# Ties in the order of work in five places of a two-layer diffusion step, and end states scaled and stored in place

## The chip, the cores and the metric

The kernel runs on one core of one Trainium2 chip. The core has five engines that each work through a queue of their own in order: TensorE (PE in the profile; PEld is its weight load), VectorE (DVE), ScalarE (ACT), GpSimd (POOL) and SyncE (SP), which here issues most of the DMAs. The metric is the device time of one execution in microseconds (us); lower is better.

## The reference

One denoising step of a backbone with two layers over 256 context tokens and 1024 latent tokens of width 1024. Layer 0 mixes tokens with gated linear attention (a scan in both directions, 4 heads, chunks of 64), layer 1 with softmax attention (8 heads, 2 key heads, normed queries and keys, rotary positions on latent tokens). Both layers are normed, modulated by a condition, gated and added to the residual. Besides the tokens it returns the end states of the context's scans and the context's keys and values. Cut to what matters:

```python
for l in range(DEPTH):
    mod_p = (silu(c_ctx) @ w_ada[l] + b_ada[l])
    mod_s = (silu(c) @ w_ada[l] + b_ada[l])
    hp = rms_norm(xp, norm_g[l]) * (1 + sc_p) + sh_p        # context; hs likewise for latent tokens
    if l % 2 == 0:
        out_p, st = gla_mixer(hp, ..., s_zero)              # st: end state of each direction and head
        out_s, _ = gla_mixer(hs, ..., state_gla)            # scans start from given states
    else:
        qp, kp, vp, gp = attn_project(hp, ...)              # k = rms_norm(k, knorm), no rotary
        out_p = (attend_blocks(qp, kp, vp) * silu(gp)) @ w_out
        out_s = (attend_blocks(rope(qs), [rope(ks), cache_k], [vs, cache_v]) * silu(gs)) @ w_out
    xp, xs = xp + gt_p * out_p, xs + gt_s * out_s
```

## The kernel before, in words

Tokens come in ten tiles of 128 rows: tiles 0 and 1 are the context, 2 to 9 the latent tokens. Every product of full precision is made of three products of 16-bit halves (`mm3`, L130): high by high, high by low, low by high. So each operand is first scaled by a power of two (`pow2`, from a maximum) and split into `hi` (ScalarE) and `lo` (VectorE).

**Who sets the order.** The text of the program is a list of instructions for each engine; before the run a planner lays out each engine's order with a timing model of its own (`schedule_with_timeline_sim`, L54), and semaphores then hold every instruction until its data are there. An instruction that stands early in its engine's order and has to wait for data holds up all behind it. `with tc.issue_after(ins):` puts every instruction of the block that runs on the engine of `ins` behind `ins` in that engine's order. It adds no wait on other engines, and instructions of the block on other engines, DMAs of SP among them, are not tied.

**The scan of layer 0** (`gla`, L824) runs 50 slots: head by head, tile by tile, forward for even heads and backward for odd ones. Each slot projects values and gates, does the work inside a chunk (`intra`), the outer product and running state (`outer`, `scan`), and for the head before it the other direction (`combine`). The running state W is a tile of a pool with two buffers (`Wa`, `Wc`). At the last context tile of a direction `final_state` (L737) scales W into the tile `s0`, which has one buffer, and ScalarE's queue stores it. The same `s0` receives the given state at the start of a scan (L727) and pieces of the gate's bias (L399). In the profile `s0` appears as `s`.

`filler` (L1558) adds other work to the slots: weights for later, and from slot 40 the output product of layer 0. `fold_gate` (L897) loads the gate vectors of a layer (two DMAs) and multiplies them by the weight's scale (eight instructions on POOL); it runs at slot 40. From slot 40 the mixed rows are loaded again in the order 2 to 9, 0, 1 (`ROWS`); `row_parts` (L928) takes a row's maximum, splits the row and turns it by DMA. Rows 2 to 7 are multiplied during the scan, at the slots of `EARLY` = 43 to 47 and 49 (`row_out`): each output tile has two halves, in the PSUM banks `A` and `kt`. `residual` (L908) evacuates a half on VectorE with two instructions: L916 scales it in the bank, L917 adds the residual to it.

**Between the layers** (`gla_out`, L943) rows 8, 9, 0 and 1 are multiplied (banks `y`), and the rows of layer 1 are normed (`norm`), turned (`turn`, banks `tr`), modulated, and made into keys and values (`key_tile`, L1122, banks `kv`). Beside that go scales of layer 1 (`att_setup`) and quarters of its output weight: `out_part` loads one into `st`, and `fill(0)` and `fill(1)` take its maxima and split it. `key_tile` norms the keys (`head_norm`), splits and turns them (`split_transpose`, with the split in the two-buffered tile `xhl`). For the two context tiles, the last of all, it also stores the keys and values.

**Attention** (`attention`, L1276) has ten steps (two groups of four heads by five chunks of 256 queries); the context chunk is the fifth in each group's first round. Each of the four heads of a step makes two blocks of scores: three-bank tiles `S`, two of them; VectorE takes the maximum (L1183, kept as `self.last`), ScalarE the exponential (L1188), POOL and VectorE split it, SP turns it into `PT`. Two heads later `values` multiplies it and L1245 evacuates it. Queries are projected two per step, ahead. In the tenth step the first output chunk is loaded, scaled and split (`out2_load`, `out2_scale`, `out2_parts`), and the first output tile multiplied in between; `att_out` (L1363) does the other nine tiles, and prepares one chunk (`out2_prep`) while the one before is multiplied. `out_tile` (L1352) loads the residual `x1_d` just ahead of its products.

Of the kernel before, what the change touches and what calls it, by code (L numbers as in the profile page):

```python
# [57 lines left out]
IDLE = (5, 9)  # L58
TURNED = 4

class K:
# [675 lines left out]
    def final_state(self, h, d, st):  # L737
        o = self.t(self.ew, [P, DV], F32, "s0", bufs=1)
        self.nc.vector.tensor_scalar(o, st["W"], st["eb"][:, d, 1:2], None, ALU.mult)
        self.nc.scalar.dma_start(self.O[2][0, 0, d, h], o)  # L740
# [75 lines left out]
    def gla_init(self):  # L816
        self.qkt = self.t(self.qkp, [P, 2 * T], F32, "qk")
        self.qk = [[[None] * 3, [None] * 3] for _ in range(GH)]
        self.inv_qk = [None, None]
        self.inv_v, self.inv_g = [None] * GH, [None] * GH  # L820
        self.v = [[None] * NT for _ in range(GH)]
        self.jobs, self.open = [], []
# [74 lines left out]
    def fold_gate(self, l, inv, gt):  # L897
        nc = self.nc
        self.gt = gt
        for i in range(2):  # L900
            nc.sync.dma_start(gt[:, i, :], self.gt_d[l, i : i + 1, :].to_broadcast([P, D]))
        for b in range(4):
            for i in range(2):
                g = gt[:, i, 256 * b : 256 * b + 256]
                nc.gpsimd.tensor_scalar(g, g, inv[b], 1.0, ALU.mult, ALU.mult)


    def residual(self, i, lhs, wo, inv, x, banks=None, cuts=(512, 512), out=None):  # L908
# [3 lines left out]
        for j, n in enumerate(cuts):  # L912
            ps = (banks[j] if banks else self.bank("y"))[:, 0:n]
            self.pieces(ps, lhs, wo, b, n)
            a = slice(b, b + n)
            nc.vector.scalar_tensor_tensor(ps, ps, inv, g[:, a], ALU.mult, ALU.mult)  # L916
            nc.vector.tensor_tensor(x[:, a], ps, x[:, a], ALU.add)  # L917
            if out is not None:
                nc.scalar.dma_start(out[:, a], x[:, a])
# [8 lines left out]
    def row_parts(self, i, parts):  # L928
        nc, og = self.nc, self.row.pop(i)
        mx = self.t(self.small, [P, 1], F32, "wm1")  # L930
        nc.vector.tensor_reduce(mx, og, AX.X, ALU.max, apply_absolute_value=True)
# [11 lines left out]
    def gla_out(self, wo, wkv):  # L943
# [32 lines left out]
        self.o1 = []  # L976
# [8 lines left out]
        with self.tc.issue_after(self.scaled):  # L985
            self.att_setup(*ckv)
# [6 lines left out]
        fill(0)  # L993
# [128 lines left out]
    def key_tile(self, i, w):  # L1122
# [4 lines left out]
        x = self.t(self.hw, [P, 2, HD], F32, "hx")  # L1127
        nc.scalar.activation(x.rearrange("p h d -> p (h d)"), ps[:, 0:256], AF.Copy, scale=self.inv_k)
        self.head_norm(x, self.kn, x)
# [3 lines left out]
        if i < NTP:  # L1133
            nc.scalar.dma_start(self.O[3][0, 0, i * P : i * P + P], x)
            v = self.t(self.hw, [P, 2, HD], F32, f"pv{i}", bufs=1)
            nc.scalar.activation(v.rearrange("p h d -> p (h d)"), pv, AF.Copy, scale=self.inv_av)
            nc.scalar.dma_start(self.O[4][0, 0, i * P : i * P + P], v)
        else:
            self.rope(x, i)
        a = slice(j * P, j * P + P)  # L1140
        self.split_transpose(x, self.asc[:, 1:2], self.kT[:, :, a])
# [91 lines left out]
    def values(self, h, c, PT, g):  # L1233
# [11 lines left out]
        nc.vector.scalar_tensor_tensor(og, o, g[1], g[0], ALU.mult, ALU.mult)  # L1245
# [30 lines left out]
    def attention(self, wo):  # L1276
# [3 lines left out]
        for n, (p, c) in enumerate(self.steps):  # L1280
# [6 lines left out]
            for e in range(4):  # L1287
# [18 lines left out]
                if n == 9 and e == 0:  # L1306
                    row = self.out2_load(OUT[0])
# [9 lines left out]
        self.out_tile(OUT[0], 0, self.t(self.sp, [P, TS + PAST], F32, "p")[:, 0:D], wo)  # L1317
        row = self.out2_load(OUT[1])
        self.second = row, *self.out2_scale(row)
        for t in pend:  # L1320
            self.values(*t, g.pop(t[0]))

# [29 lines left out]
    def out_tile(self, c, j, x, wo, cuts=(512, 512)):  # L1352
        hi, lo, inv = self.prep
        i, a = 2 * c + j, slice(j * P, j * P + P)
        self.nc.sync.dma_start(x, self.x1_d[i])
# [48 lines left out]
def emit(ctx, tc, I, O, dbg=None, stop=None):  # L1404
# [31 lines left out]
    with ExitStack() as c:  # L1436
# [119 lines left out]
        wo, part, held, rows, parts, xs, waiting = [None] * 4, [], [], [], [], [], []  # L1556

        def filler(slot):  # L1558
            if part:
# [202 lines left out]
```

## Time and profile before

| | us |
|---|---|
| median of 3 runs | 1268.66 (1267.31 to 1269.15) |
| the profiled execution | 1266.46 |
| its span | 1264.7 |
| scan and what precedes it | to about 600 |
| between the layers | about 600 to 730 |
| attention | about 730 to 1160 |
| output tiles of layer 1 | to 1260 |

The stages run into each other, so their bounds are rough. In the page and the timeline each row has its start, its length, engine and line, `out<-in`, sizes and a count; the bracket at its end tells how long the engine stood idle before it and what ended that. In the windows each row has the stretch, its length, and then the busy time and number of instructions of PE, PEld, DVE, ACT and POOL, the clock granted to TensorE (1.00 is full), the busy share of the DMA engines and the GB/s. Many `L135` rows are calls of `mm3` from different places; there the tile's name tells which.

### The profile page before, as it was taken

What the parts mean: (1) busy time and instruction counts of PE and PEld (TensorE: products, weight loads), DVE (VectorE), ACT (ScalarE), POOL (GpSimd) and SP (SyncE); (2) the same over time, 40 slices, a digit from 0 to 9 for tenths busy, and PEclk for the clock granted to TensorE, in tenths of its full rate; (3) what the DMA queues carried; (4) which work ended last, traced back from release to release, by engine and by line L of the source; (5) the groups of instructions that cost most, each with busy time, mean ns of one, the idle gap of its engine ahead of it and who ended that gap; (6) DMA issues with size and microseconds to landing.
All of it is one profiled execution on the core that took longest, in us unless ns stands there. A gap on an engine that the chain in (4) does not pass through costs nothing.

```text
span 1264.7 us, 22661 instructions
## 1 busy us (share of the span) xinstructions
PE 1212.7 (96%) x8310; PEld 810.4 (64%) x8310; DVE 887.0 (70%) x2040; ACT 593.2 (47%) x1439; POOL 402.0 (32%) x659
## 2 busy tenths in 40 slices
PE   5999999999999998989899989999999999999998
PEld 2448666655565556656688757767776766776665
DVE  5665886776688898763577678777658577795552
ACT  5564555555466666320255554444445355451010
POOL 0022222232233233300034645545344365533000
PEclk9999999999999999999999999999999999999999
DMA  9621365543444436893943166766938647668432
GB/s 356 208 101 35 109 196 151 188 146 113 128 124 137 129 113 215 262 207 112 333 151 118 26 163 154 137 139 134 213 80 201 141 92 149 134 159 214 163 124 93
DMA packets 335840, 194.42 MB, mean 154 GB/s; under 512 B 229662, under 2 KB 318606, under 8 KB 334448
## 3 DMA queue, kind: packets, MB, share of 16 engines
q1 hardware_dynamic: 293664, 159.02, 46.9%
q10 hardware_dynamic: 42064, 33.95, 8.3%
q8 instruction: 65, 1.06, 0.4%
q14 instruction: 47, 0.39, 0.1%
HBM read 103.00 MB, written 33.83 MB: 108 GB/s over the span
## 4 chain that ended last, share of the span: by engine, by line
PE 67%; DVE 14%; DMA 8%; ACT 4%; POOL 3%; issue 3%; SPq 0%; POOLq 0%; ACTq 0%; DVEq 0%
PE mm L135 35%; PE S L1180 7%; PE S L135 7%; PE A L135 2%; PE kt L135 2%; DVE wmx L157 2%; PE y L135 2%; DMA wst<-og_d 2%; PE kv L135 2%; PE A L750 2%; DMA wst<-in_gla_w_in 1%; DVE split L239 1%; POOL rope L1040 1%; DVE smx L1183 1%; PE A L691 1%
## 5 line engine op out<-in xcount | busy, mean ns | idle before, releaser
L135 PEld LDWEIGHTS <-hT_hi 128*128 128x128 f16 x1920 | 188.1, 98 | 133.6 <-issue 12.9
L135 PE MATMUL mm<-whi,hT_hi 128*128 128x512 f16 (+1 forms) x560 | 195.1, 349 | 4.3 <-DVE gx L280 2.5
L135 PE MATMUL mm<-whi,hT_lo 128*128 128x512 f16 (+1 forms) x560 | 195.3, 349 | 0.0
L135 PE MATMUL mm<-wlo,hT_hi 128*128 128x512 f16 (+1 forms) x560 | 195.2, 349 | 0.0
L135 PEld LDWEIGHTS <-whi 128*128 128x128 f16 x1344 | 131.3, 98 | 49.9 <-issue 2.9
L1204 POOL TENSOR_SCALAR phl<-p,srec 128x1280 f16<-128x1280 f32 (+1 forms) x80 | 105.4, 1317 | 167.8 <-DVE srec L1200 130.8
L1183 DVE TENSOR_REDUCE smx<-S 128x1 f32<-128x1280 f32 (+1 forms) x80 | 101.7, 1271 | 50.7 <-PE S L1180 50.7
L135 PEld LDWEIGHTS <-hT_lo 128*128 128x128 f16 x960 | 94.3, 98 | 62.1 <-issue 2.9
L135 PE MATMUL mm<-hT_hi,whi 128*128 128x256 f16 (+1 forms) x448 | 131.1, 293 | 0.0
L135 PE MATMUL mm<-hT_hi,wlo 128*128 128x256 f16 (+1 forms) x448 | 131.1, 293 | 0.0
L135 PE MATMUL mm<-hT_lo,whi 128*128 128x256 f16 (+1 forms) x448 | 131.0, 292 | 0.0
L1180 PE MATMUL S<-kT,wst 128*128 128x512 f16 (+1 forms) x624 | 122.1, 340 | 3.7 <-ACT p L1188 3.7
L1220 DVE SCALAR_TENSOR_TENSOR phl<-p,srec,phl 128x1280 f16<-128x1280 f32 (+1 forms) x80 | 107.6, 1345 | 15.0 <-POOL phl L1204 14.7
L135 PE MATMUL mm<-PT,vh 128*128 128x256 f16 x672 | 112.2, 273 | 1.8 <-DVE wlo L1347 1.2
L1188 ACT ACTIVATE p<-S,snb,sexp 128x1280 f32<-128x1280 f32 (+1 forms) x80 | 99.7, 1246 | 14.6 <-DVE phl L1220 5.2
L1180 PEld LDWEIGHTS <-wst 128*128 128x128 f16 x624 | 61.2, 98 | 54.8 <-issue 4.9
L135 PE MATMUL mm<-PT,vl 128*128 128x256 f16 x336 | 91.6, 273 | 0.0
L135 PEld LDWEIGHTS <-wlo 128*128 128x128 f16 x672 | 66.0, 98 | 24.3 <-issue 0.3
L1185 ACT ACTIVATE snb<-smx,nsexp 128x1 f32<-128x1 f32 x80 | 23.5, 293 | 110.1 <-DVE smx L1183 109.6
L135 PEld LDWEIGHTS <-vh 128*128 128x128 f16 x672 | 65.6, 98 | 10.5 <-issue 1.7
L1040 POOL TENSOR_TENSOR rope<-hx,ropet 128x64 f32<-128x64 f32 x160 | 66.2, 442 | 15.4 <-DVE hx L1043 10.3
L157 DVE TENSOR_REDUCE wmx<-wst 128x1 f32<-128x512 f32 x96 | 60.4, 674 | 7.4 <-DMA wst<-in_gla_w_in 7.4
(391 smaller groups left out, 2586.1 us busy)
## 6 DMA issues: line engine op xcount, KB each, us to landing
wada<-in_w_ada SPq DMA_DIRECT2D x13, 1024.0 KB
wst<-in_gla_w_in SPq DMA_DIRECT2D x12, 1024.0 KB
wst<-in_att_w_in SPq DMA_DIRECT2D x10, 1024.0 KB
xr<-x_d SPq DMA_DIRECT2D x15, 512.0 KB
og_d<-qk ACTq DMA_DIRECT2D x40, 128.0 KB
wst<-og_d SPq DMA_DIRECT2D x5, 1024.0 KB
out<-xr ACTq DMA_DIRECT2D x17, 256.0 KB
x<-in_x_sample SPq DMA_DIRECT2D x8, 512.0 KB
```

The costliest lines, as they stand in the source:

```text
L135: self.nc.tensor.matmul(out, a, b, start=k == 0 and j == 0, stop=k == n - 1 and j == 2)
L157: nc.vector.tensor_reduce(mx[:, j : j + 1], st[:, 2 * j : 2 * j + 2, :], AX.XY, ALU.max, apply_absolute_value=True)
L239: nc.vector.scalar_tensor_tensor(t[:, 1, v], u, s, t[:, 0, v], ALU.mult, ALU.subtract)
L691: nc.tensor.matmul(ap[:, d, :], ke[:, d, :], qe[:, d, :], start=True, stop=True)
L750: nc.tensor.matmul(o, x, y, start=j == 0, stop=j == len(terms) - 1)
L1040: nc.gpsimd.tensor_tensor(tv[:, h, :, w, :], xv[:, h, :, 1 - w, :], sn[:, :, w, :], ALU.mult)
L1180: nc.tensor.matmul(S[:, a : a + n], x, y, start=m == 0, stop=m == 2)
L1183: last = nc.vector.tensor_reduce(mx, S, AX.X, ALU.max).ins
L1185: nc.scalar.activation(nb, mx, AF.Copy, scale=self.nsexp)
L1188: nc.scalar.activation(p, S, AF.Exp, scale=self.sexp, bias=nb, accum_out=den)
L1204: nc.gpsimd.tensor_scalar(parts[:, 0:nk], p, r, 2.0 ** 14, ALU.mult, ALU.mult)
L1220: nc.vector.scalar_tensor_tensor(lo, p, r2, hi, ALU.mult, ALU.subtract)
```

## The change

Six edits. Five are about order:

1. `residual` keeps every L917 add in the list `evac`. The maxima of rows 7, 8 and 9 (`row_parts`) are tied behind the first, third and fourth of those adds (`BEHIND`): the first half of row 2 and the two halves of row 3.
2. `fold_gate` at slot 40 issues only its two loads; the eight multiplications (`fold_rest`) come at slot 43, ahead of that slot's `row_out`.
3. In `gla_out` the VectorE work of `att_setup` and of `fill(0)` of the first weight quarter is tied behind the last add of row 9.
4. `key_tile` of the context tiles leaves norm, store, split and turn of the keys to `prompt_keys`, which attention calls once in each of its first two heads, with the VectorE work tied behind the last maximum of scores. The keys wait in a part of `qk0`.
5. The first output tile's residual is loaded into two other tiles at the start of the tenth step. `out2_parts` and `out2_prep` are tied behind the first values at the tail, behind the last add, or behind the add before it.

The sixth: `final_state` scales W in place and stores from it, so `s0` is no longer used there.

```diff
+BEHIND = {7: 0, 8: 2, 9: 3}
...
     def final_state(self, h, d, st):
-        o = self.t(self.ew, [P, DV], F32, "s0", bufs=1)
-        self.nc.vector.tensor_scalar(o, st["W"], st["eb"][:, d, 1:2], None, ALU.mult)
+        o = st["W"]
+        self.nc.vector.tensor_scalar(o, o, st["eb"][:, d, 1:2], None, ALU.mult)
         self.nc.scalar.dma_start(self.O[2][0, 0, d, h], o)
...
-    def fold_gate(self, l, inv, gt):
+    def fold_gate(self, l, inv, gt, later=False):
...
+        if later:
+            return
+        self.fold_rest(inv)
+
+    def fold_rest(self, inv):
+        nc, gt = self.nc, self.gt
         for b in range(4):
...
+            xa = x[j] if isinstance(x, list) else x[:, a]
             nc.vector.scalar_tensor_tensor(ps, ps, inv, g[:, a], ALU.mult, ALU.mult)
-            nc.vector.tensor_tensor(x[:, a], ps, x[:, a], ALU.add)
+            self.evac.append(nc.vector.tensor_tensor(xa, ps, xa, ALU.add).ins)
...
-        mx = self.t(self.small, [P, 1], F32, "wm1")
-        nc.vector.tensor_reduce(mx, og, AX.X, ALU.max, apply_absolute_value=True)
+        n = BEHIND.get(i)
+        with nullcontext() if n is None else self.tc.issue_after(self.evac[n]):
+            mx = self.t(self.small, [P, 1], F32, "wm1")
+            nc.vector.tensor_reduce(mx, og, AX.X, ALU.max, apply_absolute_value=True)
...
-        with self.tc.issue_after(self.scaled):
+        with self.tc.issue_after(self.scaled), self.tc.issue_after(self.evac[-1]):
             self.att_setup(*ckv)
...
-        fill(0)
+        with self.tc.issue_after(self.evac[-1]):
+            fill(0)
...
-        x = self.t(self.hw, [P, 2, HD], F32, "hx")
+        if i < NTP:
+            x = self.qk0[:, 2048 + 256 * i : 2304 + 256 * i].rearrange("p (h d) -> p h d", h=2)
+        else:
+            x = self.t(self.hw, [P, 2, HD], F32, "hx")
...
+    def prompt_keys(self):
+        with self.tc.issue_after(self.last):
+            i, x = self.prompt.pop(0)
+            j = 10 + i
+            self.head_norm(x, self.kn, x)
+            self.nc.scalar.dma_start(self.O[3][0, 0, i * P : i * P + P], x)
+            self.split_transpose(x, self.asc[:, 1:2], self.kT[:, :, j * P : j * P + P])
...
+                if self.prompt:
+                    self.prompt_keys()
                 if len(pend) == 2:
...
                 if n == 9 and e == 0:
+                    self.first_values = None
+                    x0 = [self.t(self.hw, [P, 4, HD], F32, "hx4").rearrange("p h d -> p (h d)") for _ in range(2)]
+                    for b, t in enumerate(x0):
+                        self.nc.sync.dma_start(t, self.x1_d[2 * OUT[0], :, 512 * b : 512 * b + 512])
                     row = self.out2_load(OUT[0])
...
-        self.out_tile(OUT[0], 0, self.t(self.sp, [P, TS + PAST], F32, "p")[:, 0:D], wo)
+        self.out_tile(OUT[0], 0, x0, wo)
...
-                nxt = self.out2_prep(self.out2_load(OUT[n + 1]), to) if n else self.out2_parts(*self.second, to)
+                with self.tc.issue_after(self.evac[-1 - (n > 1)] if n else self.first_values):
+                    nxt = self.out2_prep(self.out2_load(OUT[n + 1]), to) if n else self.out2_parts(*self.second, to)
...
             if slot == FOLD:
...
-                k.fold_gate(0, [t[2] for t in wo], gt)
+                inv_wo = [t[2] for t in wo]
+                k.fold_gate(0, inv_wo, gt, True)
...
+            if slot == EARLY[0]:
+                k.fold_rest(inv_wo)
```

More of the change, by code (lines that the diff above doesn't have):

```diff
@@ L821, in gla_init @@
         self.v = [[None] * NT for _ in range(GH)]
-        self.jobs, self.open = [], []
+        self.jobs, self.open, self.evac = [], [], []
     def gla(self, wq, w, filler):
@@ L915, in residual @@
             a = slice(b, b + n)
+            xa = x[j] if isinstance(x, list) else x[:, a]
             nc.vector.scalar_tensor_tensor(ps, ps, inv, g[:, a], ALU.mult, ALU.mult)
-            nc.vector.tensor_tensor(x[:, a], ps, x[:, a], ALU.add)
+            self.evac.append(nc.vector.tensor_tensor(xa, ps, xa, ALU.add).ins)
             if out is not None:
-                nc.scalar.dma_start(out[:, a], x[:, a])
+                nc.scalar.dma_start(out[:, a], xa)
             b += n
@@ L975, in gla_out @@
                 nc.sync.dma_start(w[part], d[:, part, :, 256 * j : 256 * j + 256])
-        self.o1 = []
+        self.o1, self.prompt = [], []
         fill = self.out_part(2, self.kept2)
@@ L1126, in key_tile @@
         self.pieces(ps, lambda k: self.hT(k, i * P, P), w, 0, 512)
-        x = self.t(self.hw, [P, 2, HD], F32, "hx")
+        if i < NTP:
+            x = self.qk0[:, 2048 + 256 * i : 2304 + 256 * i].rearrange("p (h d) -> p h d", h=2)
+        else:
+            x = self.t(self.hw, [P, 2, HD], F32, "hx")
         nc.scalar.activation(x.rearrange("p h d -> p (h d)"), ps[:, 0:256], AF.Copy, scale=self.inv_k)
-        self.head_norm(x, self.kn, x)
         pv = ps[:, 256:512]
@@ L1133, in key_tile @@
         if i < NTP:
-            nc.scalar.dma_start(self.O[3][0, 0, i * P : i * P + P], x)
             v = self.t(self.hw, [P, 2, HD], F32, f"pv{i}", bufs=1)
@@ L1137, in key_tile @@
             nc.scalar.dma_start(self.O[4][0, 0, i * P : i * P + P], v)
+            self.prompt.append((i, x))
         else:
+            self.head_norm(x, self.kn, x)
             self.rope(x, i)
-        a = slice(j * P, j * P + P)
-        self.split_transpose(x, self.asc[:, 1:2], self.kT[:, :, a])
+            self.split_transpose(x, self.asc[:, 1:2], self.kT[:, :, j * P : j * P + P])
[3 more added lines that the diff above has]
+            j = 10 + i
+            self.head_norm(x, self.kn, x)
+            self.nc.scalar.dma_start(self.O[3][0, 0, i * P : i * P + P], x)
+            self.split_transpose(x, self.asc[:, 1:2], self.kT[:, :, j * P : j * P + P])
     def queries(self, i, wq, inv):
@@ L1244, in values @@
         og = self.qk0[:, 2048 + 256 * (self.io % 2) : 2304 + 256 * (self.io % 2)]
-        nc.vector.scalar_tensor_tensor(og, o, g[1], g[0], ALU.mult, ALU.mult)
+        self.vals = nc.vector.scalar_tensor_tensor(og, o, g[1], g[0], ALU.mult, ALU.mult).ins
         nc.scalar.dma_start(self.og2_d[c, :, h, :], og)
@@ L1321, in attention @@
             self.values(*t, g.pop(t[0]))
+            self.first_values = self.first_values or self.vals
     def out2_load(self, c):
@@ L1354, in out_tile @@
         i, a = 2 * c + j, slice(j * P, j * P + P)
-        self.nc.sync.dma_start(x, self.x1_d[i])
+        if not isinstance(x, list):
+            self.nc.sync.dma_start(x, self.x1_d[i])
         S = self.t(self.ps, [P, 1536], F32, "S")
@@ L1556, in emit @@
         wo, part, held, rows, parts, xs, waiting = [None] * 4, [], [], [], [], [], []
+        inv_wo = None
         def filler(slot):
+            nonlocal inv_wo
             if part:
```

## The prediction

> **What bounds the kernel now.** I read the page's busy times first, then the timeline of TensorE for every gap, then the windows for the granted clock, and last the other engines around each gap.
>
> ```profile
> span 1264.7 us, 22661 instructions
> PE 1212.7 (96%) x8310; PEld 810.4 (64%) x8310; DVE 887.0 (70%) x2040; ACT 593.2 (47%) x1439; POOL 402.0 (32%) x659
> ```
>
> TensorE is busy for 96% of the span, so all that a change of order can win is in the other 52 us. None of the matmuls is added, removed or reshaped. Eight gaps lie beside code that the diff touches (timeline of TensorE; in brackets the idle time before the row and who ended it):
>
> ```profile
> 437.54 0.70 PE L762 MATMUL o<-Sc,qe 128*128 128x256 f32 x2 [2.10 <-POOL Sc L728]
> ...
> 530.44 0.39 PE L135 MATMUL A<-whi,hT_hi 128*128 128x512 f16 x1 [2.27 <-DMA hT_hi<-parts]
> ...
> 559.43 0.58 PE L135 MATMUL A<-whi,hT_hi 128*128 128x512 f16 x1 [3.94 <-DVE p2c L102]
> ...
> 626.97 0.28 PE L135 MATMUL y<-whi,hT_hi 128*128 128x256 f16 x1 [2.83 <-DVE xr L917]
> ...
> 739.08 1.54 PE L1180 MATMUL S<-kT,wst 128*128 128x512 f16 x5 [2.67 <-ACT p L1188]
> ...
> 1159.75 0.38 PE L135 MATMUL mm<-PT,vh 128*128 128x256 f16 x2 [1.22 <-DVE wlo L1347]
> ...
> 1162.08 2.78 PE L135 MATMUL S<-kept,ropet 128*128 128x256 f16 x24 [0.64 <-DVE p L917]
> ...
> 1171.25 0.38 PE L135 MATMUL S<-whi,whi 128*128 128x512 f16 x1 [1.11 <-DVE p L917]
> ```
>
> A gap can cost more than its length. In the windows around them (the number behind POOL's bracket is the granted clock, 1.00 being full):
>
> ```profile
> 430.00:440.00 10.00, 7.90 (x41) 4.29 (x40) 8.70 (x21) 4.75 (x16) 2.09 (x5) 1.00 0.50 155
> 530.00:540.00 10.00, 9.56 (x47) 5.37 (x48) 7.38 (x27) 3.22 (x10) 2.13 (x5) 0.83 1.06 220
> 550.00:560.00 10.00, 6.06 (x53) 5.03 (x51) 7.36 (x20) 1.15 (x1) 0.00 (x0) 0.95 1.13 254
> 560.00:570.00 10.00, 10.00 (x61) 5.94 (x59) 4.33 (x8) 1.15 (x1) 0.00 (x0) 0.88 0.96 189
> 620.00:630.00 10.00, 6.60 (x34) 3.66 (x33) 8.38 (x20) 4.09 (x8) 2.27 (x4) 0.86 1.10 345
> 630.00:640.00 10.00, 10.00 (x68) 6.75 (x67) 4.93 (x12) 2.04 (x4) 2.15 (x4) 0.97 0.55 203
> 735.00:740.00 5.00, 2.33 (x16) 1.32 (x15) 1.39 (x4) 3.17 (x8) 0.67 (x1) 0.99 0.85 240
> 740.00:745.00 5.00, 5.00 (x31) 3.59 (x30) 3.80 (x7) 3.30 (x11) 4.67 (x9) 0.67 0.36 82
> ```
>
> What the clock withheld is window length times (1 - clock): behind the gap at 530 it is 10 x 0.17 = 1.7 us; at 559, 10 x 0.05 + 10 x 0.12 = 1.7; at 627, 1.4 + 0.3 = 1.7; at 739, 5 x 0.01 + 5 x 0.33 = 1.7. The gap of 2.10 at 437 cost none. So four of the gaps cost their length and 1.7 us each.
>
> [...]
>
> **The change part by part.**
>
> *Rows 7, 8 and 9 behind the evacuations (BEHIND).* TensorE's last product into bank A for row 3, and VectorE's order after it:
>
> ```profile
> 548.72 0.38 PE L135 MATMUL A<-whi,hT_lo 128*128 128x512 f16 x1
> 550.29 1.22 DVE L931 TENSOR_REDUCE wm<-wst 128x1 f32<-128x1024 f32 x1 [2.05 <-DMA wst<-og_d]
> ...
> 555.51 1.22 DVE L931 TENSOR_REDUCE wm<-wst 128x1 f32<-128x1024 f32 x1 [2.29 <-DMA wst<-og_d]
> ...
> 558.69 0.68 DVE L917 TENSOR_TENSOR whi<-A,whi 128x512 f32<-128x512 f32 x1
> ```
>
> The bank was full at 549.1 and emptied at 559.4, because VectorE stood twice behind a row's maximum whose data had not landed (2.05 and 2.29 us). With the ties the two maxima queue behind the adds of row 3; they are wanted only by rows 8 and 9, whose output tiles belong to the next stage. Bank A is then free near 551, before TensorE asks at 555.5. Gain 3.94 + 1.7 = **5.6 us**.
>
> *fold_gate split in two.* It moves eight POOL instructions from slot 40 to slot 43.
>
> ```profile
> L905 POOL TENSOR_SCALAR wst<-wst,p2i x8: 469/474/1602, 524.3 to 529.8; 128x256 f32<-128x256 f32 x8
> ...
> 526.23 1.35 SPq L937 DMA_TRANSPOSE hT_hi<-parts  x1
> ...
> 528.36 0.44 DVE L114 TENSOR_TENSOR ors<-ors,half_g 128x1 f32<-128x1 f32 x1 [2.57 <-POOL ors L126]
> ```
>
> VectorE's wait of 2.57 us for POOL should go. TensorE's gap at 530 hangs on the transpose that SP issued at 526.23, and neither the transpose nor SP's queue ahead of it is touched. From below I bound this part at -3.8 us (eight at 0.474, all of them in front of the first evacuation with nothing beside them), from above at 2.27 + 1.7 = 4.0. I take **0**, the nearest row being the transpose's. Its two DMAs stay at slot 40, so nothing moves on SP.
>
> *att_setup and fill(0) behind out(9).* VectorE around the gap at 627:
>
> ```profile
> 624.44 1.87 DVE L157 TENSOR_REDUCE wmx<-st 128x1 f32<-128x512 f32 x3
> 626.23 0.68 DVE L917 TENSOR_TENSOR xr<-y,xr 128x512 f32<-128x512 f32 x1
> ...
> 654.19 2.47 DVE L157 TENSOR_REDUCE wmx<-st 128x1 f32<-128x512 f32 x4 [1.08 <-DMA st<-in_att_w_out]
> ```
>
> Four maxima over a weight (three of them in the first row) stand between the two halves of an evacuation. Four take 2.47 us by the last row, so L917 could start near 623.8 and TensorE 2.45 us earlier. Gain 2.45 + 1.7 = 4.15. But the four (2.5 us) and the five short reductions of att_setup now come when VectorE has the latent tiles to turn, and the second load into the same buffer starts that much later; at 654 VectorE already waits 1.08 us for it, in front of work that TensorE needs. Between nothing and 2.5 us of this comes back; I take 1.5, nearer the upper end because that wait is on record. Net **2.65 us**.
>
> *Prompt keys put off into attention.* ScalarE and VectorE at the start of attention, then POOL, and a window of the same stage:
>
> ```profile
> 732.97 0.61 DVE L1029 SCALAR_TENSOR_TENSOR hx<-hx,hrs,kn 128x128 f32<-128x128 f32 x2 [1.52 <-POOL hrs L126]
> 733.50 1.48 DVE L1183 TENSOR_REDUCE smx<-S 128x1 f32<-128x1280 f32 x1
> ...
> 737.33 0.48 DVE L1057 SCALAR_TENSOR_TENSOR xhl<-hx,asc,xhl 128x256 f16<-128x256 f32 x1 [2.35 <-ACT xhl L1056]
> ...
> 736.79 0.51 ACT L1056 ACTIVATE xhl<-hx,asc 128x256 f16<-128x256 f32 x1 [4.91 <-DMA wst<-xhl]
> ...
> 732.24 0.70 POOL L126 TENSOR_TENSOR hrs<-hrsa,mhalf 128x2 f32<-128x2 f32 x1
> ...
> 741.01 1.82 POOL L126 TENSOR_TENSOR hrs<-hrsa,mhalf 128x2 f32<-128x2 f32 x1
> ...
> 745.00:750.00 5.00, 5.00 (x37) 3.33 (x35) 5.00 (x7) 2.77 (x6) 3.46 (x5) 1.00 0.23 52
> ```
>
> The maximum of the first scores was there at 735.0, but ScalarE stood 4.91 us in front of the split of a prompt tile, whose buffer was still being transposed, and was done with it at 737.3. Without that split in front it turns to the scores 2.3 us earlier, and TensorE, idle since 736.4, goes on at about 736.8. Gain 2.3 + 1.7 = 4.0. The two tiles' work comes back a little later: VectorE 2 x (0.61 + 0.48) = 2.2 us, ScalarE's squares and splits, POOL's powers and two transposes on SP, in front of the next maxima. VectorE has no idle time from 745 to 750, so 0 to 3.5 us of it may reach TensorE. I take 2.0, about VectorE's share. Net **2.0 us**.
>
> [...] A prompt tile's power took 0.70 us at 732 and a query's 1.82 at 741, with VectorE in its scores. [...]
>
> *The tail of attention.* Two rows of VectorE:
>
> ```profile
> 1161.33 0.69 DVE L917 TENSOR_TENSOR p<-S,p 128x512 f32<-128x512 f32 x1 [1.20 <-DMA p<-x_d]
> ...
> 1167.17 2.34 DVE L1335 TENSOR_REDUCE wmx<-wst 128x1 f32<-128x1024 f32 x2 [5.15 <-DMA wst<-og_d]
> ```
>
> Each gap is an evacuation that stands behind something: the first values behind the split L1347 (gap 1.22), an add behind its residual's late load (0.64), and one behind a maximum that waits 5.15 us for its load (1.11). The new ties and the early load of x0 turn all three round. What is put off, the second chunk's preparation, is wanted two output tiles later, about 20 us. Gain **2.9 us**; TensorE runs on to the end, so this part is hard to lose again.
>
> *End states in place.* The state's store and the next state's load share one buffer:
>
> ```profile
> 429.57 0.36 ACTq L740 DMA_DIRECT2D out<-s  x1
> 434.69 5.88 SPq L727 DMA_DIRECT2D s<-in_state_gla  x3
> ```
>
> The load leaves SP 5.1 us after the store was issued, when the buffer is free; POOL's scaling waits for it, and TensorE 2.10 us for POOL. Without the shared buffer the load goes early. Now W, two buffers, is held for those 5.1 us; the same buffer is asked for again two slots later, behind two whole projections. Gain **2.1 us**; without that cover W would stall VectorE up to 5.1 us, which would cost the 2.1 and up to 3.0 more. I take the full gain, since the row of the gap itself names the load.
>
> **Sum.** 5.6 + 0 + 2.65 + 2.0 + 2.9 + 2.1 = 15.25, say 15 us. The profiled execution took 1266.46 us (its span and 1.8 us around it) and the median of the three runs shown is 1268.66; off the median that gives **1253.5 us** (off the profiled one 1251.3).
>
> **The rivals.**
>
> - *The fold frees the gap at 530 too, or the give-backs stay away*: 4.0, or 1.5 + 2.0 more: 19 us, 1249.7. For it: VectorE's 2.57 us. Against it: the transpose. Chance 0.15.
> - *Everything at 627 and 739 comes back*, in the new work that VectorE does there: 10.6 us, 1258. For it: VectorE full from 745 to 750. Chance 0.18.
> - *The clock still drops at 627 and 739*: shortened gaps of about 0.4 us with others beside them trip it again. 15 - 3.4 = 11.6, 1257. [...] Chance 0.08; the uncharged gap of 2.10 at 437 speaks against it.
> - *The ties do not do it*: the planner that lays out every engine's order answers each tie with another instruction that waits for a DMA in front of the same evacuation, and the gaps only move. 1267 to 1271. Chance 0.08.
> - *Slower: ScalarE is blocked inside attention.* The prompt splits need the buffers that also serve the queries, and SP's queue now holds the long transposes:
>
> ```profile
> 759.61 12.58 SPq L1221 DMA_TRANSPOSE PT<-phl  x3
> ```
>
> If a split stands at ScalarE's head until such a run is through, the exponentials stand with it and TensorE runs out of banks: 12.6 + 1.7 for each of two tiles, 28.6 us less the 15 won: 1282. It decides for slower once each split waits over 7.6 us; the wait on record is 4.91. Chance 0.11.
>
> **How the numbers follow.** The forecast has 0.40. Faster by over 0.2% (2.5 us, about what a measurement of this kernel can tell from no change) are the forecast and the first three rivals, 0.81; within it the fourth, 0.08; slower 0.11. The range runs from 1246 (all give-backs away and the fold's 4.0, 22.7 us) to 1265, which takes in the part-gains and leaves out the last two rivals; the fold at -3.8 and W at -3.0 end inside it (1257.3, 1258.6).
>
> **What would show it.** Right: no gap over 1 us in front of bank A, y, or the third scores, and clock 1.00 in the windows behind them; L931 of rows 8 and 9 after L917 of row 3; ScalarE's first exponential directly after the first maximum; the state's load seconds before its POOL instruction; TensorE without a gap in the last 100 us; a gap still at bank A's first product. Wrong: VectorE waiting for the weight `st` in front of a turned tile, a split waiting for `xhl` in front of an exponential, or new gaps in the scan, where only the in-place state alters anything.

## The result, and the profile after

| | before | after |
|---|---|---|
| median | 1268.91 us (1267.31 to 1269.97) | 1254.63 us (1252.12 to 1255.48) |
| ratio, 95% interval | | 0.9885 [0.9867, 0.9904] |
| the profiled execution | 1266.46 us | 1255.37 us |

The ratios go by the fast executions alone: one of 4467 us, of the earlier weight split without the row ties, counts in its median and not in its ratio.

The forecast was 1253.5 us. The page of the changed kernel begins, in the lines that were shown of before:

```profile
span 1253.6 us, 22651 instructions
...
PE 1208.6 (96%) x8310; PEld 810.0 (65%) x8310; DVE 887.9 (71%) x2040; ACT 593.1 (47%) x1439; POOL 404.1 (32%) x659
```

The instruction counts of the engines are unchanged; TensorE's busy time fell by 4.1 us and its idle time by 7. Busy time can fall without less work: at a lowered clock fewer matmuls fill the same window (43 at 0.71 against 71 at 1.00 in the windows below). By the windows that accounts for 1.7 us of the 4.1: 6.8 us were withheld before (four times 1.7, by the prediction), 5.1 here (3.4 in these windows, 1.7 near 266). The rest was not traced. The gaps that are left beside the changed places, and one that is new in the scan (timeline of TensorE, changed kernel; its line numbers stand 1 to 30 higher than those of before):

```profile
446.31 0.38 PE L136 MATMUL mm<-whi,hT_hi 128*128 128x512 f16 x1 [1.92 <-ACT gx L631]
...
529.89 0.61 PE L136 MATMUL A<-whi,hT_hi 128*128 128x512 f16 x1 [3.63 <-DMA hT_hi<-parts]
...
617.92 0.33 PE L446 MATMUL tr<-ident,xr 128*128 128x128 f32 x1 [1.11 <-DVE xr L441]
...
635.30 0.23 PE L94 MATMUL kv<-ident,amx 128*128 128x128 bf16 x1 [1.92 <-DVE wm L162]
...
1146.83 1.36 PE L136 MATMUL S<-kept,ropet 128*128 128x256 f16 x11 [1.54 <-DVE p2c L103]
```

The gaps at 437, 559, 627, 739, 1160 and 1171 are gone or under 1 us. The one at bank A's first product, 2.27 before, is now 3.63, and the windows around it show the clock (the number behind POOL's bracket):

```profile
520.00:530.00 10.00, 5.92 (x50) 4.81 (x48) 7.28 (x23) 3.46 (x7) 7.84 (x12) 0.95 1.04 223
530.00:540.00 10.00, 10.00 (x43) 5.12 (x43) 7.25 (x31) 3.70 (x10) 1.89 (x4) 0.71 1.10 240
540.00:550.00 10.00, 10.00 (x71) 6.67 (x70) 8.39 (x14) 2.78 (x3) 0.00 (x0) 1.00 0.88 180
```

It withheld 0.5 + 2.9 = 3.4 us, twice what the same gap cost before.

To compare kernels by stage I took from TensorE's timeline the start of the first matmul into a bank (bank A for row 2, bank y, the first scores, the first values, the first output tile) and the end of the last matmul. All in us; the second row of the changed kernel is another execution, on the chip of the last experiments.

| profiled execution | A starts at | A to y | y to scores | scores to values | values to output | to the end |
|---|---|---|---|---|---|---|
| before | 530.44 | 76.69 | 120.15 | 30.84 | 384.80 | 117.29 |
| after | 529.89 | 71.15 | 118.71 | 25.71 | 388.00 | 115.64 |
| after, again | 528.28 | 71.05 | 118.99 | 26.31 | 386.92 | 115.74 |
| row ties alone | 530.83 | 69.73 | 119.03 | 28.52 | 384.76 | 117.82 |
| no row ties | 527.14 | 71.79 | 117.47 | 27.63 | 387.43 | 118.03 |
| fold at slot 40 | 526.08 | 72.08 | 119.59 | 26.31 | 385.87 | 115.94 |
| no ties behind row 9 | 530.48 | 70.87 | 126.11 | 25.71 | 386.22 | 115.59 |
| prompt keys in `key_tile` | 528.97 | 70.04 | 117.39 | 32.42 | 384.86 | 116.58 |
| tail of before | 528.87 | 69.61 | 117.59 | 26.32 | 385.91 | 118.99 |
| states by `s0` | 530.95 | 69.77 | 120.67 | 26.53 | 385.99 | 118.10 |
| earlier weight split | 528.17 | 70.18 | 114.37 | 25.72 | 386.32 | 116.23 |
| the same, no row ties | 527.18 | 79.20 | 114.34 | 25.92 | 386.83 | 117.73 |
| cache loads first | 526.12 | 70.08 | 115.67 | 25.72 | 387.15 | 116.58 |
| both | 524.69 | 70.39 | 114.34 | 25.71 | 386.43 | 116.26 |

The first column differs by 1.6 us between the two executions of the changed kernel (529.89 and 528.28), and 1.4 of that is there already at the scan's last cumulative sum (479.54 and 478.17). The first execution lost 1.7 us of clock near 266, ahead of all the tied places; the second did not, nor did the kernel before (the last section shows it). So the second is the one to hold against the kernel before in that column. The other columns of the two agree within about 1.

### The profile page after: what moved, and what is told of

Its sections match the earlier page's. It is cut to its first block, busy times and chain, and to the rows that moved or that the text cites. A ratio compares the mean times of both kernels' runs of the same rounds, so it can differ in the third digit from the quotient of the medians.

```text
span 1253.6 us, 22651 instructions
## 1 busy us (share of the span) xinstructions
PE 1208.6 (96%) x8310; PEld 810.0 (65%) x8310; DVE 887.9 (71%) x2040; ACT 593.1 (47%) x1439; POOL 404.1 (32%) x659
```

## The experiments

The median of the kernel before lay between 1267.15 and 1267.86 us beside these runs. Each ratio is to it.

**The changed kernel without the row ties.**

```diff
-BEHIND = {7: 0, 8: 2, 9: 3}
+BEHIND = {}
```

> The changed kernel with the ties of rows 7, 8 and 9 taken out alone. Theory 1 (each place is worth its gap and the clock behind it, whatever stands elsewhere): the gap of about 3.9 us at bank A's product for row 4 comes back, with a granted clock under 1.00 behind it, 5.6 us more: about 1260. Theory 2 (the places are coupled by DMAs: the stage between the layers starts when its transposes land, so time won in the scan is waited away there): the gap comes back, but the first product into bank y moves by under 3 us and the end by less than that: 1255 to 1257.

Measured: 1252.19 us, ratio 0.9874 [0.9839, 0.9908], below what either theory expected. Taking the largest term of the forecast away cost nothing that can be told. Its timeline of TensorE says where the gap went:

```profile
527.14 0.39 PE L136 MATMUL A<-whi,hT_hi 128*128 128x512 f16 x1 [1.53 <-DMA hT_hi<-parts]
...
542.63 0.38 PE L136 MATMUL A<-whi,hT_hi 128*128 128x512 f16 x1 [2.33 <-DVE whi L925]
```

A gap behind an add is back at bank A (2.33), and the one at bank A's first product is 2.1 us shorter. Together they are 3.86, against 3.63 with the ties. The two maxima of rows 8 and 9 stand in front of the add again, but here they wait 0.82 and 0.17 us for their data, not the 2.05 and 2.29 of before.

**The row ties alone, in the kernel before.** The list `evac` and the tied maxima, nothing else.

```diff
+BEHIND = {7: 0, 8: 2, 9: 3}
...
+        n = BEHIND.get(i)
+        with nullcontext() if n is None else self.tc.issue_after(self.evac[n]):
```

> The kernel before with the ties of rows 7, 8 and 9 (BEHIND) and nothing else. Theory of the prediction: the gap of 3.94 us at bank A's row 4 and 1.7 us of clock behind it go, 5.6 us: about 1263, ratio 0.9955. Rival (bank A's products are paced by something else as well, so that what the ties free is lost by the first y product, as undoing them in the changed kernel suggests): the gap goes, but the time from bank A's first product to the first y product (76.7 us before) shrinks by less than 2 us, and the ratio is 0.998 to 1.000.

Measured: 1256.52 us, ratio 0.9919 [0.9896, 0.9943]: 10.3 us, more than either expected, and over two thirds of the whole change. From A to y it is 7.0 us shorter (76.69 to 69.73), which is the gap of 3.94 and nearly all of the 3.4 us of clock behind it and behind the gap at 530. The 1.7 us behind the gap at 530 are not the ties' doing: that gap is still there, 2.58 us long, and cost no clock in this execution. And 2.3 us more came where no edit was made, from scores to values. Three rows of it, two of TensorE and one of ScalarE:

```profile
530.83 0.39 PE L136 MATMUL A<-whi,hT_hi 128*128 128x512 f16 x1 [2.58 <-DMA hT_hi<-parts]
...
729.06 1.24 PE L1183 MATMUL S<-kT,wst 128*128 128x512 f16 x5 [0.45 <-ACT p L1191]
```

```profile
726.70 0.51 ACT L1059 ACTIVATE xhl<-hx,asc 128x256 f16<-128x256 f32 x1 [2.66 <-DMA wst<-xhl]
```

The prompt tile's split, which stood 4.91 us in front of the first exponential, stands 2.66 here with `key_tile` unchanged, and the gap of 2.67 that I had given to the prompt keys is 0.45. The gap at the second half of the y banks went too: VectorE's order around it was laid out anew.

```profile
616.41 0.68 DVE L918 TENSOR_TENSOR xr<-y,xr 128x512 f32<-128x512 f32 x1
...
619.86 2.46 DVE L158 TENSOR_REDUCE wmx<-st 128x1 f32<-128x512 f32 x4 [2.69 <-DMA st<-in_att_w_out]
```

The four maxima over `st` stand behind the add here, without a tie. So three gaps that I had priced to three edits are gone with the first alone.

**fold_gate whole at slot 40.**

```diff
-                k.fold_gate(0, inv_wo, gt, True)
+                k.fold_gate(0, inv_wo, gt)
...
-            if slot == EARLY[0]:
-                k.fold_rest(inv_wo)
```

> The changed kernel with all of fold_gate at slot 40 again. Theory 1: 0, 1254 to 1255, since TensorE's wait at bank A's first product hangs on a transpose. Theory 2: POOL's eight instructions in front of the running state's scaling cost as much there as at slot 43, also 0. Rival: the late multiplications are what frees the scan's tail, 2 to 4 us more, 1257 to 1259.

Measured: 1251.35 us, ratio 0.9872 [0.9842, 0.9903]: no difference that can be told. POOL in the changed kernel, then in this one:

```profile
523.34 5.75 POOL L912 TENSOR_SCALAR wst<-wst,p2i 128x256 f32<-128x256 f32 x8 [2.01 <-DMA w_o<-split]
529.09 0.54 POOL L731 TENSOR_SCALAR Sc<-Wc,eb,eb 128x256 f32<-128x256 f32 x1
```

```profile
520.81 5.47 POOL L912 TENSOR_SCALAR wst<-wst,p2i 128x256 f32<-128x256 f32 x8 [2.30 <-DMA w_o<-split]
526.27 0.55 POOL L731 TENSOR_SCALAR Sc<-Wc,eb,eb 128x256 f32<-128x256 f32 x1
```

In both the eight instructions stand in one run, in front of the same scaling of the running state. Where they stand in the text of the program made no difference to POOL's order.

**No ties of `att_setup` and `fill(0)` behind row 9.**

```diff
-        with self.tc.issue_after(self.scaled), self.tc.issue_after(self.evac[-1]):
+        with self.tc.issue_after(self.scaled):
             self.att_setup(*ckv)
...
-        with self.tc.issue_after(self.evac[-1]):
-            fill(0)
+        fill(0)
```

> The changed kernel without the ties of att_setup and fill(0) behind row 9's last add. Theory 1: the gap of 2 to 3 us at bank y comes back with its clock, less the new wait of 1.92 us for att_setup's matmul, which goes: 1.5 to 2.6 us more, 1256 to 1257.5. Theory 2: the maxima over the cache wait for a load that lands at a fixed time, so the order around them is worth nothing: 1253 to 1255.

Measured: 1258.67 us, ratio 0.9928 [0.9903, 0.9954], above what either theory expected. From y to scores it takes 7.4 us more (126.11), and yet the gap at y stays away. VectorE shows another:

```profile
634.68 1.36 DVE L1092 TENSOR_REDUCE amx<-hx 128x1 f32<-128x512 f32 x2 [7.20 <-DMA hx<-in_cache_k]
```

It stands 7.20 us in front of a maximum over the cached keys, which `att_setup` takes and on which the scales of the first key product hang. TensorE waits for it:

```profile
636.16 0.50 PE L94 MATMUL kv<-ident,amx 128*128 128x128 bf16 x3 [5.08 <-DVE amx L1095]
```

The gap is 3.2 us longer than the 1.92 with the ties, and behind it the clock withheld 3.4 us (2.6 from 630 to 640, 0.8 from 640 to 650), of which the changed kernel lost none in one execution and 1.7 in the other. Together that is 6.6 of the 7.4. So the ties are worth some 3 us of gap in this company and what clock goes with it; they are not what closed the gap that they were made for.

**Prompt keys in `key_tile` again.**

```diff
-        if i < NTP:
-            x = self.qk0[:, 2048 + 256 * i : 2304 + 256 * i].rearrange("p (h d) -> p h d", h=2)
-        else:
-            x = self.t(self.hw, [P, 2, HD], F32, "hx")
+        x = self.t(self.hw, [P, 2, HD], F32, "hx")
...
-            self.prompt.append((i, x))
```

and the norm, store, split and turn at their place of before.

> Prompt keys normed, stored, split and turned in key_tile again; all else as in the changed kernel (1254.63 us, ratio 0.9885 to the kernel before). Theory (each place is worth its own gap and the clock behind it): the third scores wait for ScalarE again, a gap of 2 to 3 us near 730 with the clock down behind it; 2 to 4 us slower than the changed kernel, 1256.5 to 1258.5, ratio 0.990 to 0.992. Rival (the work put off comes back in full in the first heads of attention): within 1 us of the changed kernel, with the interval from last kv product to first values equally long in both, ratio 0.988 to 0.9895.

Measured: 1256.18 us, ratio 0.9915 [0.9887, 0.9944]. The ratio is where theory put it, but its interval overlaps that of the changed kernel; the stages decide. Scores to values 32.42 instead of 25.71 and 26.31, values to output 384.86 instead of 388.00 and 386.92. TensorE, then ScalarE:

```profile
729.77 1.56 PE L1199 MATMUL S<-kT,wst 128*128 128x512 f16 x6 [3.25 <-ACT p L1207]
```

```profile
727.81 0.51 ACT L1067 ACTIVATE xhl<-hx,asc 128x256 f16<-128x256 f32 x1 [0.94 <-DMA wst<-xhl]
728.23 1.40 ACT L1207 ACTIVATE p<-S,snb,sexp 128x1280 f32<-128x1280 f32 x1
```

The split stands in front of the first exponential again. With the prompt keys put off, 6.1 to 6.7 us are won at the start of attention, 1.7 of them clock that was withheld here behind the gap of 3.25 (0.66 from 730 to 735), and 2.1 to 3.1 are lost again inside attention. Some 1.5 us more are lost from y to scores, which takes 117.39 here. Not all that is lost inside attention need be the put-off work: in the first execution of the changed kernel a gap of 1.83 us stands at 905, some 160 us behind it, that this kernel does not have.

**The tail of before.** No early load of the residual, no ties of the second chunk.

```diff
...
-        self.out_tile(OUT[0], 0, x0, wo)
+        self.out_tile(OUT[0], 0, self.t(self.sp, [P, TS + PAST], F32, "p")[:, 0:D], wo)
...
-                with self.tc.issue_after(self.evac[-1 - (n > 1)] if n else self.first_values):
+                with nullcontext():
```

> The tail of attention as before: residual of the first output tile loaded late, no ties of out2_parts and out2_prep. Theory: the gaps of 1.22, 0.64 and 1.11 us near the first values at the tail and the first output tiles come back, while the one of 1.54 us that the changed kernel shows in front of its first output tile goes; 1.4 to 2.9 us slower, 1256 to 1257.5, ratio 0.9895 to 0.991, all of it after the last scores. Rival (the put-off split at the tail costs what the ties win, as the remaining gap in front of the second half shows): within 0.7 us of the changed kernel, ratio 0.988 to 0.9895.

Measured: 1253.50 us, ratio 0.9883 [0.9861, 0.9905], no difference in the time. In the trace the last stage is 3.3 us longer than in the changed kernel (118.99). The gaps that were expected are there, 2.66 us in place of 1.54:

```profile
1144.90 0.38 PE L136 MATMUL mm<-PT,vh 128*128 128x256 f16 x2 [0.99 <-DMA PT<-phl]
1147.16 2.78 PE L136 MATMUL S<-kept,ropet 128*128 128x256 f16 x24 [0.57 <-DVE p L925]
1156.33 0.38 PE L136 MATMUL S<-whi,whi 128*128 128x512 f16 x1 [1.10 <-DVE p L925]
```

and so is one of 1.30 at 1173, which neither the kernel before nor the changed one has. The 3.3 us are made up elsewhere, in code that is the same: 1.4 to 1.5 from A to y (1.7 us of clock withheld at bank A instead of 3.4), 1.1 to 1.4 from y to scores, 1.0 to 2.1 inside attention. Rival and theory each hold by one of the two measures. By the time, the tail's ties have no worth that can be told; the interval leaves room for up to some 3 us.

**End states through `s0` again, with the five ties.**

```diff
-        o = st["W"]
-        self.nc.vector.tensor_scalar(o, o, st["eb"][:, d, 1:2], None, ALU.mult)
+        o = self.t(self.ew, [P, DV], F32, "s0", bufs=1)
+        self.nc.vector.tensor_scalar(o, st["W"], st["eb"][:, d, 1:2], None, ALU.mult)
```

> The changed kernel with the end states scaled into s0 again (the five ties alone). Theory 1: the gap of about 2 us in the scan comes back: 1256.7. Theory 2: the scan is 2 to 3.5 us longer up to its last slots, but bank A's first product waits for row 2's transpose, which lands at the same time, so the end moves by under 0.6 us; and if the gap there is shorter the clock drops less, which may give 1.7 us back: 1253 to 1255.

Measured: 1257.80 us, ratio 0.9920 [0.9891, 0.9949]; the interval overlaps that of the changed kernel, so again the stages decide. TensorE shows the gap of before, and a small one at bank A:

```profile
438.76 0.70 PE L763 MATMUL o<-Sc,qe 128*128 128x256 f32 x2 [2.21 <-POOL Sc L729]
...
530.95 0.39 PE L136 MATMUL A<-whi,hT_hi 128*128 128x512 f16 x1 [1.77 <-DMA hT_hi<-parts]
```

In the changed kernel the load of that state, the sixth of eight, left SP 133 us earlier than here (435.94), and POOL's scaling of it waited for nothing:

```profile
303.09 0.34 SPq L728 DMA_DIRECT2D s<-in_state_gla  x1
...
405.45 0.47 POOL L729 TENSOR_SCALAR Sc<-s,eb 128x256 f32<-128x256 f32 x1
```

TensorE's last cumulative sum of the scan starts at 484.25 here, at 479.54 and 478.17 in the changed kernel: 4.7 to 6.1 us, and 4.7 against the execution that lost the same 1.7 us of clock near 266 as this one. (All kernels here with states in place have it between 476.81 and 480.50, the three with `s0` between 483.05 and 484.25.) At bank A's first product only 1.1 to 2.7 of it are left, because what comes last there is the turn of row 2, and TensorE now waits 3.63 and 3.53 us for it instead of 1.77. The rest of the difference in time lies behind y (a gap of 4.38 us at the first key product, 2.42 in the last stage) and was not taken apart.

**Two places that limit the changed kernel.** In front of the turn of row 2, ScalarE of the changed kernel shows:

```profile
513.67 1.33 ACT L239 ACTIVATE split<-wst,p2s 128x512 f16<-128x512 f32 x2 [5.22 <-DMA w_o<-split]
```

That is the last of the weight pieces that `filler` has split ahead and stored to `w_o`, at the slots listed in `AHEAD`. The first experiment puts it two slots earlier:

```diff
-AHEAD = (2, 7, 9, 11, 12, 17, 19, 20, 22, 27, 30, 37)
+AHEAD = (2, 7, 9, 11, 12, 17, 19, 20, 22, 27, 30, 35)
```

> The changed kernel with the last weight quarter of layer 0 split two slots earlier (last slot of AHEAD 37 to 35), so that ScalarE and the DMA queues are free when row 2 is split. Theory: the gap at bank A's first product (3.63 us, 3.4 us of clock behind it) is set by how late the split and the turns of row 2 start on ScalarE and SP, and shrinks to under 2 us with the clock kept: 3 to 5 us faster, 1249.5 to 1251.5, ratio 0.985 to 0.986. Rival (the turns land late because the DMA engines are full, share 1.04, whenever they are issued): gap 3 to 4 us as before, time within 1 us, ratio 0.988 to 0.9895.

Measured: 1245.33 us, ratio 0.9823 [0.9802, 0.9843]; nearly 8 us faster than the changed kernel, and more than expected. The gap at bank A's first product is gone, but not by an earlier start. SP issued the turn in the changed kernel, and in this one, at:

```profile
523.79 0.33 SPq L1664 DMA_DIRECT2D split<-in_x_sample  x1
524.17 1.71 SPq L947 DMA_TRANSPOSE hT_hi<-parts  x1
```

```profile
508.54 0.34 SPq L1664 DMA_DIRECT2D split<-in_x_sample  x1
...
524.81 1.35 SPq L947 DMA_TRANSPOSE hT_hi<-parts  x1
```

It landed 5.7 us after its issue in the one (529.89) and no more than 3.4 in the other (528.17). The window fits the rival: the busy share of the DMA engines, last but one, is 0.51 instead of 1.04. The rows above name a part of what filled them: a load of 512 KB into the tile `split`, with which SP waited 4.4 us until the weight piece's stores had left that tile. It goes right ahead of the turn in the changed kernel and 16 us ahead of it here.

```profile
520.00:530.00 10.00, 8.53 (x80) 6.79 (x81) 8.71 (x33) 5.41 (x11) 5.74 (x12) 1.00 0.51 120
```

So these two traces speak for the rival's mechanism, full DMA engines, and not for an earlier start; but which transfers fill them there can be changed. No run moved that load alone. Nor is all of TensorE's waiting gone: gaps of 1.35 at 512 and 1.81 at 521 stand ahead of bank A in this kernel. From the scan's last cumulative sum to bank A it takes 47.67 us, against 50.35 and 50.11. The largest part of the gain, 4.3 us, lies from y to scores. SP of the changed kernel:

```profile
616.53 5.00 SPq L947 DMA_TRANSPOSE hT_lo<-wlo  x1
627.42 0.34 SPq L250 DMA_DIRECT2D wlo<-w_q  x1
627.86 0.55 SPq L1082 DMA_DIRECT2D hx<-in_cache_k  x1
```

The cache loads stand behind a load that SP holds from 621.5 to 627.4, and VectorE waits for them:

```profile
627.44 2.45 DVE L158 TENSOR_REDUCE wmx<-st 128x1 f32<-128x512 f32 x4
633.81 1.36 DVE L1093 TENSOR_REDUCE amx<-hx 128x1 f32<-128x512 f32 x2 [3.92 <-DMA hx<-in_cache_k]
```

With the earlier weight split SP reaches the same load at 608.24, and VectorE does not wait. The second experiment puts the cache loads ahead of it and leaves the weight split:

```diff
+        self.cached = nc.sync.dma_start(cv, I["cache_v"][0, 0].rearrange("(t p) h d -> p t h d", p=P)).ins
...
-        with self.tc.issue_after(self.scaled):
+        with self.tc.issue_after(self.scaled), self.tc.issue_after(self.cached):
             self.wq = [self.load_w("q0", 2)]
```

> The changed kernel with the loads of the cached keys and values put on SP ahead of the load of the first query weight, which waits there for a split. Theory (what came back between the layers is SP's queue, which held the cache load, on which VectorE stood 3.92 us in front of the modulation of the first keys): the gap of 1.92 us at the first kv product goes; 1.9 us faster, up to 3.6 with clock, 1251 to 1253, ratio 0.985 to 0.987. Rival (VectorE has too much to do there whatever the order of SP): a gap of 1.5 to 3 us stays at the first kv product, ended by VectorE; ratio 0.988 to 0.9895.

Measured: 1249.60 us, ratio 0.9860 [0.9836, 0.9885]. The gap at the first key product is gone and the stage takes 115.67. The ratio is where theory put it; its interval still overlaps that of the changed kernel, so the stage shows it and the time alone does not.

**The earlier weight split, without the row ties.**

```diff
-BEHIND = {7: 0, 8: 2, 9: 3}
+BEHIND = {}
```

> The kernel with the last weight quarter split two slots earlier (1245.33 us), here without the ties of rows 7, 8 and 9. Theory (undoing the ties cost nothing in the changed kernel only because the gap of 3.63 us at bank A's first product and its clock came and went with them): with that gap gone, a gap of 2 to 4 us behind the adds of row 3 and 1.7 us of clock come back, 1249 to 1251, ratio 0.985 to 0.9865. Rival (the ties have no worth here at all): within 1 us of that kernel, ratio 0.9815 to 0.983.

Measured: 1253.73 us, ratio 0.9876 [0.9850, 0.9903], against 0.9823 with the ties: some 6.7 us by the ratios, more than the 4 to 6 expected. Beside the one left out, its executions spread from 1247.33 to 1257.46 us, and the profiled one took 1257.46, so the stages below show more than the mean. From A to y it takes 9.0 more, by gaps at bank A and at `kt` and 1.7 us of clock (0.79 from 585 to 590, 0.87 from 590 to 595):

```profile
543.68 0.38 PE L136 MATMUL A<-whi,hT_hi 128*128 128x512 f16 x1 [2.12 <-DVE p2e L105]
...
587.51 0.28 PE L136 MATMUL kt<-whi,hT_hi 128*128 128x256 f16 x1 [4.99 <-DVE whi L925]
```

The same ties that could be left out of the changed kernel at no cost that can be told are needed once the gap in front of them is closed.

**The changed kernel again, and both new edits together.**

> The changed kernel once more, on the chip of the runs beside it, as their reference: 1252 to 1256 us, ratio 0.987 to 0.990, with a gap of 2.3 to 3.7 us at bank A's first product.

Measured: 1253.58 us, ratio 0.9886 [0.9868, 0.9904], with gaps of 3.53 us at bank A and 2.35 at the first key product.

> The earlier split of the last weight quarter and the cache loads put first on SP, together. Theory (two places, two gaps): gains add up except what the first already took of the gap at the first kv product (1.92 us): 1243 to 1245, ratio 0.980 to 0.982. Rival (the second is worth nothing once the first has moved VectorE's work there): 1245 to 1246, ratio 0.982 to 0.983.

Measured: 1244.53 us, ratio 0.9814 [0.9797, 0.9831]. It beats both kernels. Beside the earlier weight split alone (0.9823) no gain can be told, and from y to scores it takes 114.34 against 114.37: the rival held there, since the earlier split had already brought the cache loads forward.

## Why the prediction was right in the sum and not in its terms

The forecast of 1253.5 us against 1254.63 is right, and the largest term, the row ties, has its mechanism shown. That the sum comes within 1 us is luck in part: several terms were off, some too high and some too low. Its terms by stage, against the two profiled executions of the changed kernel (differences of the table above):

| stage | predicted | measured | again |
|---|---|---|---|
| to bank A's first product (states, fold) | -2.1 | -0.55 | -2.16 |
| A to y (row ties) | -5.6 | -5.54 | -5.64 |
| y to scores (ties behind row 9) | -2.65 | -1.44 | -1.16 |
| scores to values (prompt keys) | -4.0 | -5.13 | -4.53 |
| values to output (give-back) | +2.0 | +3.20 | +2.12 |
| to the end (tail) | -2.9 | -1.65 | -1.55 |
| sum | -15.25 | -11.11 | -12.92 |

The medians differ by 14.3; the profiled execution of the kernel before, 1266.46, was faster than its median, 1268.91. Without the 1.7 us of clock lost near 266 the -0.55 of the first row would be about -2.2. Step by step:

- **Row ties.** The step was right: the maxima of rows 8 and 9 stand behind the adds, and bank A is free in time. VectorE of the changed kernel:

```profile
550.99 0.68 DVE L925 TENSOR_TENSOR whi<-A,whi 128x512 f32<-128x512 f32 x1
551.59 1.21 DVE L941 TENSOR_REDUCE wm<-wst 128x1 f32<-128x1024 f32 x1
```

  The stage's 5.54 agrees with 5.6 only in sum. The ties alone shorten it by 7.0; the changed kernel pays 2.9 of withheld clock there, of the gap in front, and the kernel before paid 3.4.
- **fold_gate.** The price of 0 held. "VectorE's wait of 2.57 us for POOL should go" was wrong: VectorE still waits 2.73 us there, for the running state's scaling behind the eight multiplications, and does so with `fold_gate` whole at slot 40 too. POOL's order is the planner's, and the new place in the text did not change it.
- **The gap at 530 stays as it is.** This is the step that failed. I had argued that nothing in front of the turn of row 2 was touched. That is true, but TensorE comes there 1.9 and 3.4 us earlier in the two executions, and the gap grew from 2.27 us to 3.63 and 3.53; the clock behind it withheld 3.4 instead of 1.7. With the clock that is 3.1 and 3.0 us more, most of what the end states won. How much of it the clock takes does not go by the gap's length alone (with the tail of before a gap of 3.49 there cost 1.7; see the last section).
- **End states in place.** Mechanism right (the load goes early, the gap at 437 is gone, VectorE was not stalled by W), size wrong on both sides. By the last cumulative sum 3.5 and 4.9 us are won (483.05 to 479.54 and 478.17), and 4.9 is the figure of the executions without the clock loss near 266, over twice the 2.1 forecast; 0.55 and 2.2 are left at bank A. That the second equals the forecast is luck. The prediction had named new gaps in the scan as a sign against it: one came, 1.92 us at 446, and gaps of 1.53 at 448 and 1.22 at 476 went. Where the rest was won was not followed.
- **att_setup and fill(0).** The gap of 2.83 and its clock went, but 2.7 and 3.0 us of the 4.15 came back, not the 1.5 taken. In the first execution the gaps of 1.11 at 617 and 1.92 at 635 are that much, and the larger hangs on the cache loads on SP and not on the weight `st`, the place that I had named.
- **Prompt keys.** Right in both halves: in the changed kernel ScalarE turns to the first scores as soon as VectorE has their maximum, and 2.1 to 3.2 us come back inside attention (with the gap at 905 in the larger figure). But the ties of the rows alone close the gap of 2.67 too, so it was not the prompt keys' alone to win. Had each moved power of POOL grown from the 0.70 us at 732 to the 1.82 at 741, the give-back would have been 4.2, by an estimate from these two rows (2.0 and twice 1.1). One in four took that long: 0.70 and 0.70 us in one execution, 1.99 and 0.69 in the other; why was not shown. The two prompt splits (L1067, at 737.2 and 747.2) waited for nothing, so the rival of 1282 did not come about. ScalarE, after:

```profile
724.78 0.29 ACT L1206 ACTIVATE snb<-smx,nsexp 128x1 f32<-128x1 f32 x1 [0.92 <-DVE smx L1204]
```

- **The tail.** The three gaps went, and one of 1.54 us took their place: the evacuation of the first output tile stands behind two splits of probabilities that wait for POOL. VectorE, after:

```profile
1143.77 1.55 DVE L1241 SCALAR_TENSOR_TENSOR phl<-p,srec,phl 128x1280 f16<-128x1280 f32 x1 [1.23 <-POOL phl L1225]
1145.24 0.75 DVE L924 SCALAR_TENSOR_TENSOR S<-S,p2i,wst 128x512 f32<-128x512 f32 x1
```

- **The sum itself.** It treated six places as independent. They are not: the row ties alone bring 10.3 us [7.2, 13.2], the changed kernel with all six edits 14.3, and the changed kernel without the row ties still 16.0 by its ratio, 11.7 to 20.4 by its interval. Where the planner's order and the landing of DMAs carry on into the next stage, an edit early on moves the gaps of later ones. How the planner came to each new order was not followed.

## What to carry to other kernels

A gap that an edit leaves alone is not a constant: if TensorE reaches it earlier and it ends with a transfer, it can take back part of what was won before it (here 1.4 of 1.9 us and 1.3 of 3.4), so look for the next transfer behind every gain. An edit undone at no cost may still be the one that brought the time; try it alone in the old kernel, and again once the next limit is gone. Where a planner lays out the order, a new place in the text is not a new place in a queue, and a gap may close without the tie made for it.

## What was not expected of the hardware

In these executions the clock withheld behind a gap came as nothing, 1.7 or 3.4 us, and the length of the gap alone did not decide which. Two pairs of windows show it for the gap at bank A's first product, of the row ties alone (a gap of 2.58 us) and of the fold at slot 40 (2.65):

```profile
520.00:530.00 10.00, 8.25 (x71) 5.99 (x70) 6.88 (x19) 4.18 (x9) 6.00 (x10) 1.00 0.67 196
530.00:540.00 10.00, 9.08 (x56) 5.58 (x57) 7.04 (x23) 3.14 (x9) 2.08 (x5) 1.00 1.09 223
```

```profile
520.00:530.00 10.00, 6.59 (x45) 4.77 (x44) 7.22 (x22) 3.78 (x10) 6.52 (x10) 0.84 0.99 244
530.00:540.00 10.00, 10.00 (x56) 5.78 (x54) 7.27 (x23) 2.96 (x6) 1.75 (x3) 0.82 0.88 191
```

The gap of 2.58 us cost nothing, the one of 2.65 cost 1.6 + 1.8 = 3.4; with the tail of before the gap there was 3.49 and cost 0.9 + 0.8 = 1.7 (clock 0.91 from 520 to 530, 0.92 from 530 to 540). A gap near 266, in the scan and ahead of all ties, shows the same within one kernel. First the changed kernel, then its second execution:

```profile
266.03 1.12 PE L708 MATMUL U<-v,ks 128*128 128x256 f32 x2 [2.09 <-ACT v L624]
...
260.00:270.00 10.00, 7.91 (x47) 4.56 (x46) 9.36 (x24) 7.60 (x21) 3.04 (x6) 0.83 0.87 272
```

```profile
265.85 0.70 PE L708 MATMUL U<-v,ks 128*128 128x256 f32 x2 [1.76 <-ACT v L624]
...
260.00:270.00 10.00, 8.24 (x56) 4.61 (x54) 9.36 (x23) 7.42 (x21) 2.85 (x6) 1.00 0.86 280
```

2.09 us cost 1.7 and 1.76 nothing; in the kernel before the same gap is longer, 2.27, and cost nothing (clock 1.00 from 260 to 280). And the gap at 437, which was free before at 2.10, cost 1.7 at 2.07 with the row ties alone (clock 0.71 from 435 to 440, 0.95 from 440 to 445). In the prediction each gap near 2.5 us was charged 1.7; for a single gap in a single execution that can be wrong by 1.7 either way. What decides between nothing, 1.7 and 3.4 us was not shown: no run here moved a single gap and left the rest in place.
